# A planner's prices for VectorE and ScalarE, its page lines, and the order of a tail product

## The chip, the cores and the metric

The kernel runs on one core of one Trainium2 chip. The metric is the device time in microseconds of one execution; the median of several is given. The profile is taken by the hardware in one execution of its own.

## The reference

One decoder layer on a sequence of 512 tokens with 1024 features, all float32. What is computed, cut to its skeleton:

```python
h = rms_norm(x, mix_norm_g)
u, q, kv, nsa_g, merge_g = split(h @ w_in)
gate_pool, gate_nsa = split(sigmoid(merge_g))
y_pool = pooling_mixer(u) @ w_pool_out          # causal means over 2, 4, 8, 16 tokens
y_nsa = nsa_mixer(q, kv, sigmoid(nsa_g)) @ w_nsa_out   # compressed, selected and window attention
x = x + (gate_pool * y_pool + gate_nsa * y_nsa) @ w_out
h = rms_norm(x, ffn_norm_g)
gate_pre, val = split(h @ w_up)                 # 1024 -> 2 x 2816
x = x + (silu(causal_dwconv(gate_pre)) * val) @ w_down # 2816 -> 1024
```

## The kernel before

**Arithmetic.** Features lie on the 128 partitions, tokens along the free dimension. Every float32 operand of a large product is split in a high part (rounded, `hi`) and a rest (`lo`), and a product is three matmuls: hi x hi, hi x lo, lo x hi. `split` makes both by a ScalarE copy and a VectorE subtraction. `split_by_dma` makes the rest by a negated ScalarE copy and a DMA on POOL's queue that adds the original to it, and the high part by a second ScalarE copy.

**Stages.** Up to 38 us of the profile the q and k projections. From there to about 258 us attention runs in one stream of TensorE's program ("m") and the pooling, gates and their projections in another ("f"). Then, in one stream, the output projection of attention, `w_out`, and the feed-forward part, whose 22 feature tiles of 128 are called f: the first three plain, the others by `up_fast`, which replaces eight products of half size by seven (a Strassen-like scheme; `seven` prepares the seven weight operands by sums, `product` multiplies 256 token columns by four k tiles of 128). Parts of the down projection (`fill`) lie in between. The last eight down tiles are done two at a time by four calls of `seven_into`, p = 0 to 3, over the feature tiles 14 to 21: this is the tail. The moving operands of its products are `yq`, `yh` and `yl` of single tiles, or `zh` and `zl`, sums of pairs; k = 3 is the pair of the tiles 20 and 21, the last that `up_fast` makes. In `seven_into` the product with `h1` goes into a bank `bq`, the one with `h2` is added to a bank `by`. Each of them is then taken by VectorE into an output tile (`add`), and both banks are used again.

**Order.** Nothing is emitted as the program is written. `Plan` first records every operation (`note`), with a price (`price`: time on the engine `cost`, time after that until its result is there `tail`, bytes of a DMA `land`) and its dependences. `run` then simulates the engines with a list scheduler: for each engine, of the operations that could start within 0.12 us of the earliest, the one with the least key goes first. TensorE's operations stay in the order of their stream, and only the two streams are interleaved. DMAs share an assumed rate. Operations wait until the tiles that they open (`allocs`) have a buffer. Pages are 56 buffers of 128 x 512 float32, from which most tiles are taken; the staging tiles of `seven` (made by `soon`) are taken in a fixed order, a line, kept by `early`. `dues` then goes back over the plan and gives each operation the latest time at which it doesn't delay TensorE (`due`), which is the key of the next round. `search` does 12 rounds, and the plan with the least sum of four trial executions under other DMA assumptions is emitted; its order of instructions for each engine and its buffers are then fixed for the chip. All instructions are issued from one line of `emit`, so all carry the line L431 in the profile; tiles tell them apart.

Of the kernel before, what the change touches and what calls it, by code (L numbers as in the profile page):

```python
# [86 lines left out]
def _cols(x):  # L87
    n = 1
    for _, c in list(x.ap)[1:]:
        n *= c  # L90
    return n


class Op:
    __slots__ = ("i", "eng", "calls", "cost", "tail", "land", "deps", "succ", "allocs", "tiles", "stream", "left",
                 "ready", "start", "fin", "due", "hand", "port")

    def __init__(self, i, eng, stream):
        self.i, self.eng, self.stream = i, eng, stream
# [15 lines left out]
class Plan:  # L115
# [54 lines left out]
    def note(self, eng, method, a, kw):  # L170
        if self.open is None or self.open == "new":
            op = Op(len(self.ops), eng, self.stream)
            op.deps.update(o.i for o in self.after)
            self.ops.append(op)
            if self.open == "new":
                self.open = op
            if method == "transpose":
                op.cost += SWITCH
        else:
            op = self.open  # L180
            assert op.eng == eng
        outs = [a[0]] if a else []
        outs += [v for k, v in kw.items() if k in self.OUT and v is not None]
        ins = [v for v in a[1:] if hasattr(v, "tensor")]
        ins += [v for k, v in kw.items() if k not in self.OUT and hasattr(v, "tensor")]
        op.calls.append((method, a, kw))
        cost, tail, land = self.price(eng, method, outs, ins, a, kw)
        op.cost += cost
        op.port |= eng == "POOL" and method[:6] == "tensor" or eng == "DVE" and not any(
            x.tensor.name in self.psum for x in ins)  # L190
        op.tail = tail
        op.land = max(op.land, land)
        if kw.get("accum_op") is not None:
            ins.append(outs[0])
        for x, w in [(x, False) for x in ins] + [(x, True) for x in outs]:
            n = x.tensor.name
            if n not in self.tag:
                continue
            r = (0, 999, 0, 1 << 30) if n in self.psum and n not in self.fine else _span(x)
            past = list(self.writes.get(n, ()))  # L200
            if w:
                past += self.reads.get(n, ())
            for o, q in past:
                if o is not op and r[0] < q[1] and q[0] < r[1] and r[2] < q[3] and q[2] < r[3]:
                    op.deps.add(o.i)
            (self.writes if w else self.reads).setdefault(n, []).append((op, r))
            if not self.users[n]:
                op.allocs.append(n)
            if op not in self.users[n][-1:]:
                self.users[n].append(op)  # L210

    def price(self, eng, method, outs, ins, a, kw):
        n = max(_cols(x) for x in outs + ins)
        if method == "dma_start":
            x = outs[0]
            size = x.ap[0][1] * _cols(x) * 4 if hasattr(x, "ap") else 0
            return (0.87 if eng == "POOL" else 0.45), 0.0, size * (1.75 if kw.get("accum_op") is not None else 1.0)
        if eng == "PE":
            n = _cols(a[2])
            c = max(n / 2250.0 + (0.005 if n < 300 else 0.0), 0.109)  # L220
            return c * (2 if method == "matmul" and a[1].dtype == F32 else 1), 0.17, 0
        if eng == "ACT":
            c = 0.19 + n * 0.000835
            if any(_cols(x) == 1 for x in ins):
                c += 0.09
            if kw.get("accum_out") is not None:
                c += 0.19
            if a[2] in (AF.Sin,):
                c += 1.28
            return c, 0.0, 0  # L230
        if eng == "DVE":
            wide = [x for x in ins if _cols(x) > 1]
            if method == "tensor_tensor_reduce":
                return 0.24 + n * 0.00105, 0.0, 0
            if len(wide) > 1 or method == "tensor_reduce" or any(x.tensor.name in self.psum for x in wide):
                return 0.15 + n * (0.00105 if method != "scalar_tensor_tensor" else 0.00114), 0.0, 0
            return 0.2 + n * 0.00054, 0.0, 0
        if method == "memset":
            return 0.1 + n * 0.0008, 0.0, 0
        return 0.12 + n * 0.0023, 0.0, 0  # L240

    def run(self, key, reserve, land, rate=RATE, extra=EXTRA, fixed=None):
# [1 line left out]
        ahead = 0 if fixed else AHEAD  # L244
        engs = ("PE", "ACT", "DVE", "POOL", "SP")
        free = {t: [(0.0, "", i) for i in range(c)] for t, c in self.caps.items()}
        slot = self.slot if fixed else {}
        nxt = {t: 0 for t in self.FIFO}
        left = {n: len(u) for n, u in self.users.items()}
        clock = dict.fromkeys(engs, 0.0)  # L250
# [3 lines left out]
        pool = {e: [] for e in engs}  # L254
        heads = {}
        for o in ops:
            o.left, o.ready, o.start, o.hand = len(o.deps), 0.0, None, []
            if o.eng == "PE":
                heads.setdefault(o.stream, []).append(o)
            elif not o.left:  # L260
                pool[o.eng].append(o)
# [5 lines left out]
        def finish(o):  # L267
            for n in o.tiles:
                left[n] -= 1
                if not left[n]:  # L270
                    free[self.tag[n]].append((max(u.fin for u in self.users[n]) + 0.06, n, slot[n][1]))
            for s in o.succ:
                s.left -= 1
                s.ready = max(s.ready, o.start + o.cost if s.eng == o.eng and not o.land else o.fin + 0.06)
                if not s.left and s.eng != "PE":
                    pool[s.eng].append(s)

# [20 lines left out]
        def when(o):  # L298
            t, seen = o.ready, {}
            for n in o.allocs:  # L300
                g = self.tag[n]
                seen[g] = k = seen.get(g, 0) + 1
                f = free[g]
                if fixed:
                    past = [x[0] for x in f if x[1:] == slot[n]]
                    if not past:
                        return None
                    t = max(t, past[0])
                    continue
                if g in nxt and self.rank[n] != nxt[g] or n in self.early and self.early[n] != line[0]:  # L310
                    return None
                if len(f) < k + (0 if g != "pg" else ahead if n in self.early else reserve if o.stream == "f" else 0):
                    return None
                t = max(t, min(f)[0] if k == 1 else sorted(f)[k - 1][0])
            return max(t, clock[o.eng], port[0] if o.port and o.eng != port[1] else 0.0)
# [25 lines left out]
        while len(order) < len(ops):  # L341
# [9 lines left out]
            w, o = best  # L351
# [12 lines left out]
            else:  # L364
                pool[o.eng].remove(o)
            for n in o.allocs:
                g = self.tag[n]
                f = free[g]
                past = [x for x in f if x[1:] == slot[n]][0] if fixed else min(f)
                slot[n] = past[1:]  # L370
                f.remove(past)
                for u in self.users.get(past[1], ()):
                    u.hand.append(o)
                if g in nxt:
                    nxt[g] += 1
                if n in self.early:
                    line[0] += 1
            order.append(o)
            if not o.land:
                finish(o)  # L380
# [6 lines left out]
    def dues(self, order):  # L387
        lost, end, due = 0.0, 0.0, {}
        for o in order:
            if o.eng == "PE":  # L390
                lost += max(0.0, o.start - end)
                end = o.start + o.cost
                due[o.i] = o.start - lost + self.base
        for o in reversed(order):
            d = due.get(o.i, 1e9)
            for s in o.succ + o.hand:
                d = min(d, s.due - 0.06 - (o.fin - o.start))
            o.due = d

    def search(self, tries, reserve):  # L400
        for n, u in self.users.items():
# [33 lines left out]
def hybrid_layer(ctx: ExitStack, tc: tile.TileContext, found, first, xT, pos, par, cst, poolw, w1, wa, wb, wf,  # L435
# [695 lines left out]
        n = x.ap[1][1]  # L1131
        return bass.AP(tensor=x.tensor, offset=x.offset + n - 1, ap=[list(x.ap[0]), [-1, n]])

    def product(bank_, a, b, k0, nk=4):
        ah, al = a
        bh, bl = b
        for k in range(nk):
            c = slice(k * P, (k + 1) * P)
            with pl.unit():
                for j, (w, x) in enumerate(((ah, bh), (ah, bl), (al, bh))):  # L1140
                    PE.matmul(back(bank_[:, :H2]), w[:, c], back(x(k)), start=k0 and k == 0 and j == 0,
                              stop=k == nk - 1 and j == 2, skip_group_check=True)
# [61 lines left out]
    def seven_into(o0, o1, w, mv, nk, done, last):  # L1204
# [10 lines left out]

        def rest():
            bq = any_bank()
            product(bq, h1, mv(2, 0), True, nk)
            add(o1, HI, bq, -1)
            product(by, h2, mv(2, 1), False, nk)  # L1220
            add(o0, HI, by, 1)
            product(bx, a12, mv(1, 0), False, nk)
            add(o0, LO, bx, 1)
# [369 lines left out]
```

## Time and profile before

| what | value |
|---|---|
| median of 3 runs | 681.88 us (681.45 to 682.67) |
| the profiled execution | 682.61 us |
| its span | 680.7 us |
| TensorE busy | 675.9 us (99%), 4182 matmuls |
| VectorE, ScalarE busy | 515.4 us (1095), 451.8 us (848) |
| granted TensorE clock | 0.999 |

The span goes from the first to the last instruction of the program; the execution's time has 1.9 us more. PE is TensorE's matmul, PEld its weight load, DVE VectorE, ACT ScalarE, POOL GpSimd, SP SyncE, which issues most loads. Names such as `sl<-r` say output and input by the program's tiles. A matmul's duration overlaps the next one's, so whether TensorE waits is read from the distance between starts: 0.227 us for 512 columns and 0.118 us for 256 where nothing is waited for.

### The profile page before, as it was taken

The page shows a single profiled execution, that of the slowest core. Times are in us where ns is not written, and L with a number is a line of the kernel's source. Part 1 is how long each engine was busy: PE and PEld are TensorE (multiplying, and loading weights), DVE is VectorE, ACT ScalarE, POOL GpSimd, SP SyncE. Part 2 cuts the span into 40 slices and gives each one's busy share as a digit, 9 for nine tenths or more (in the row PEclk, how much of TensorE's full clock was granted, in tenths as well). Part 3 has the DMA queues.
Part 4 walks back from the last instruction along what each step waited for, and adds up shares of the span by engine and source line. Part 5 has one row for each costly group of instructions (what it writes and reads, how often), then busy time and mean ns, then how long its engine had stood idle before and what let it go on. Part 6 is the DMA issues. An engine that isn't in the chain of part 4 may idle for free.

```text
span 680.7 us, 11651 instructions
## 1 busy us (share of the span) xinstructions
PE 675.9 (99%) x4182; PEld 607.3 (89%) x4182; DVE 515.4 (76%) x1095; ACT 451.8 (66%) x848; POOL 117.4 (17%) x142
## 2 busy tenths in 40 slices
PE   9999999999999999999999999999999999999998
PEld 8898888888888888888888999999999999999997
DVE  6869878888888743876879977866677777888882
ACT  8565878777766653444758877866666667778770
POOL 0012211000111110000203432322222223222240
PEclk9999999999999999999999999999999999999999
DMA  8466995425556558736739798887677767878882
GB/s 304 145 167 166 268 250 141 109 63 155 125 125 155 143 120 274 281 126 231 186 87 234 139 224 214 176 215 168 155 164 188 185 163 167 187 165 193 185 175 92
DMA packets 50586, 119.28 MB, mean 175 GB/s; under 512 B 5856, under 2 KB 7904, under 8 KB 50528
## 3 DMA queue, kind: packets, MB, share of 16 engines
q0 software_dynamic: 18432, 40.90, 34.4%
q1 hardware_dynamic: 31808, 77.36, 34.0%
q8 instruction: 33, 0.54, 0.3%
q10 hardware_dynamic: 288, 0.27, 0.1%
q14 instruction: 25, 0.20, 0.1%
HBM read 70.27 MB, written 6.29 MB: 112 GB/s over the span
## 4 chain that ended last, share of the span: by engine, by line
PE 96%; DMA 2%; issue 1%; DVE 0%; POOL 0%; SPq 0%; POOLq 0%
PE mm L431 38%; PE tr L431 33%; PE sc L431 13%; PE av L431 13%; DMA sl<-r 1%; DMA wraw<-wa 0%; POOL sl L431 0%; DVE th L431 0%; DVE u L431 0%; DVE wraw L431 0%; DVE x L431 0%; SPq L431 0%; DVE whi L431 0%; POOLq L431 0%; DVE y L431 0%
## 5 line engine op out<-in xcount | busy, mean ns | idle before, releaser
L431 ACT ACTIVATE whi<-wraw 128x1024 fp32r<-128x1024 f32 (+1 forms) x89 | 90.4, 1019 | 66.9 <-issue 23.0
L431 DVE TENSOR_TENSOR wlo<-wraw,whi 128x1024 fp32r<-128x1024 f32 (+1 forms) x62 | 71.4, 1154 | 18.7 <-ACT whi L431 18.2
L431 POOL DMA_DIRECT2D sl<-r x46 | 40.0, 869 | 226.2 <-ACT sl L431 212.8
L431 PE MATMUL mm<-xh,whi 128*128 128x512 f32 x176 | 70.3, 400 | 0.1
L431 PE MATMUL mm<-xh,wlo 128*128 128x512 f32 x176 | 68.9, 391 | 0.0
L431 PE MATMUL mm<-xl,whi 128*128 128x512 f32 x176 | 68.8, 391 | 0.0
L431 POOL DMA_DIRECT2D wlo<-wraw x28 | 24.5, 876 | 246.9 <-ACT wlo L431 194.2
L431 PE MATMUL tr<-nh,whi 128*128 128x256 f32 x216 | 46.6, 282 | 0.0
L431 ACT ACTIVATE wlo<-wraw 128x1024 fp32r<-128x1024 f32 x28 | 29.5, 1059 | 24.2 <-PE mm L431 22.9
L431 ACT ACTIVATE pp<-pp,asm 128x128 f32<-128x128 f32 (+3 forms) x64 | 35.6, 558 | 13.9 <-DVE asm L431 13.3
L431 DVE SCALAR_TENSOR_TENSOR ft<-fg,pr,ft 128x511 f32<-128x511 f32 (+1 forms) x44 | 33.0, 750 | 12.7 <-ACT ft L431 11.8
L431 PE MATMUL tr<-nh,wlo 128*128 128x256 f32 x144 | 40.5, 282 | 0.0
L431 PEld LDWEIGHTS mm<-xh,wlo 128*128 128x128 f32 x176 | 33.0, 188 | 7.3
L431 PEld LDWEIGHTS mm<-xh,whi 128*128 128x128 f32 x176 | 33.1, 188 | 5.6 <-DVE u L431 0.5
L431 PEld LDWEIGHTS mm<-xl,whi 128*128 128x128 f32 x176 | 33.1, 188 | 5.0
L431 PEld LDWEIGHTS tr<-nh,whi 128*128 128x128 f32 x216 | 35.6, 188 | 0.0
L431 PE MATMUL sc<-yh,whi 128*128 128x512 f32 x91 | 35.5, 390 | 0.0
L431 PE MATMUL sc<-yl,whi 128*128 128x512 f32 x91 | 35.5, 390 | 0.0
L431 PE MATMUL sc<-yh,wlo 128*128 128x512 f32 x91 | 35.4, 389 | 0.0
L431 PE MATMUL tr<-tl,sh 128*128 128x256 f32 x113 | 31.8, 281 | 0.0
L431 ACT ACTIVATE sh<-wraw 128x512 fp32r<-128x512 f32 x44 | 27.4, 622 | 4.3 <-DVE wraw L431 4.1
L431 ACT ACTIVATE sl<-r 128x512 fp32r<-128x512 f32 x46 | 28.6, 622 | 2.0 <-DVE r L431 1.0
(451 smaller groups left out, 2261.5 us busy)
## 6 DMA issues: line engine op xcount, KB each, us to landing
wlo<-wraw POOLq DMA_DIRECT2D x28, 512.0 KB, 4.7
wraw<-wup SPq DMA_DIRECT2D x24, 512.0 KB, 4.0
sl<-r POOLq DMA_DIRECT2D x46, 256.0 KB, 4.5
wraw<-wf SPq DMA_DIRECT2D x22, 512.0 KB, 3.7
r<-wup SPq DMA_DIRECT2D x38, 256.0 KB, 5.2
sl<-s POOLq DMA_DIRECT2D x23, 256.0 KB, 4.6
sl<-wraw POOLq DMA_DIRECT2D x22, 256.0 KB, 4.5
wraw<-wout SPq DMA_DIRECT2D x8, 512.0 KB, 3.7
```

The source lines that it names most:

```text
L431: getattr(self.real[o.eng], method)(*a, **kw)
```

## The change

Three parts.

1. `price` for ScalarE and VectorE. Before, an operation held its engine for its whole duration and had no tail; a dependent one on the same engine could start when that cost was over. Now the cost is the step from one start to the next, about 0.1 (ScalarE) or 0.085 us (VectorE) shorter than the duration, and that rest is the tail. A dependent operation on the same engine starts 0.035 us after the end, TensorE's excepted. Operands of one column are priced each, and the custom reduction and the three-operand form are no longer priced apart.
2. Page lines. A tile is opened by any operation that meets no earlier access of it, not by the first recorded one alone, and once only (`got`). Operations that take a page of the line (`lined`) inherit in `dues` the earliest due time of later ones in the line.
3. `product` can be given its k tiles. In `seven_into`, where there is no earlier group's end to place (p = 0), the products with `h1` and `h2` do their first three k tiles each, then the fourth of each, and the subtraction from `o1` follows both.

The core of the diff:

```diff
-            if not self.users[n]:
+            if not met and n not in op.allocs:
                 op.allocs.append(n)
...
+        few = sum(_cols(x) == 1 for x in ins)
         if eng == "ACT":
-            c = 0.19 + n * 0.000835
-            if any(_cols(x) == 1 for x in ins):
-                c += 0.09
-            if kw.get("accum_out") is not None:
-                c += 0.19
+            c = 0.19 + n * 0.00085 + 0.095 * few
             if a[2] in (AF.Sin,):
                 c += 1.28
-            return c, 0.0, 0
+            if kw.get("accum_out") is not None:
+                return 0.30 + n * 0.0008, 0.2, 0
+            over = 0.115 if any(x.tensor.name in self.psum for x in ins) else 0.1
+            return c - over, over, 0
         if eng == "DVE":
             wide = [x for x in ins if _cols(x) > 1]
-            if method == "tensor_tensor_reduce":
-                return 0.24 + n * 0.00105, 0.0, 0
+            c = 0.155 + 0.06 * few
             if len(wide) > 1 or method == "tensor_reduce" or any(x.tensor.name in self.psum for x in wide):
-                return 0.15 + n * (0.00105 if method != "scalar_tensor_tensor" else 0.00114), 0.0, 0
-            return 0.2 + n * 0.00054, 0.0, 0
+                c += n * 0.00105
+            else:
+                c += n * 0.00054
+            return c - 0.085, 0.085, 0
...
-                s.ready = max(s.ready, o.start + o.cost if s.eng == o.eng and not o.land else o.fin + 0.06)
+                s.ready = max(s.ready, o.fin + 0.06 if s.eng != o.eng or o.land else o.start + o.cost if o.eng == "PE" else o.fin + 0.035)
...
+        line = 1e9
         for o in reversed(order):
             d = due.get(o.i, 1e9)
+            if o.lined:
+                d = min(d, line)
             for s in o.succ + o.hand:
                 d = min(d, s.due - 0.06 - (o.fin - o.start))
             o.due = d
+            if o.lined:
+                line = d
...
-            product(bq, h1, mv(2, 0), True, nk)
-            add(o1, HI, bq, -1)
-            product(by, h2, mv(2, 1), False, nk)
+            if last:
+                product(bq, h1, mv(2, 0), True, nk)
+                add(o1, HI, bq, -1)
+                product(by, h2, mv(2, 1), False, nk)
+            else:
+                for ks in (range(nk - 1), (nk - 1,)):
+                    product(bq, h1, mv(2, 0), True, nk, ks)
+                    product(by, h2, mv(2, 1), False, nk, ks)
+                add(o1, HI, bq, -1)
```

More of the change, by code (lines that the diff above doesn't have):

```diff
@@ L95 @@
     __slots__ = ("i", "eng", "calls", "cost", "tail", "land", "deps", "succ", "allocs", "tiles", "stream", "left",
-                 "ready", "start", "fin", "due", "hand", "port")
+                 "ready", "start", "fin", "due", "hand", "port", "lined")
     def __init__(self, i, eng, stream):
@@ L202, in note @@
                 past += self.reads.get(n, ())
-            for o, q in past:
-                if o is not op and r[0] < q[1] and q[0] < r[1] and r[2] < q[3] and q[2] < r[3]:
-                    op.deps.add(o.i)
+            met = [o for o, q in past if r[0] < q[1] and q[0] < r[1] and r[2] < q[3] and q[2] < r[3]]
+            op.deps.update(o.i for o in met if o is not op)
             (self.writes if w else self.reads).setdefault(n, []).append((op, r))
-            if not self.users[n]:
+            if not met and n not in op.allocs:
                 op.allocs.append(n)
@@ L246, in run @@
         free = {t: [(0.0, "", i) for i in range(c)] for t, c in self.caps.items()}
-        slot = self.slot if fixed else {}
+        slot, got = self.slot if fixed else {}, set()
         nxt = {t: 0 for t in self.FIFO}
@@ L256, in run @@
         for o in ops:
-            o.left, o.ready, o.start, o.hand = len(o.deps), 0.0, None, []
+            o.left, o.ready, o.start, o.hand, o.lined = len(o.deps), 0.0, None, [], False
             if o.eng == "PE":
@@ L300, in when @@
             for n in o.allocs:
+                if n in got:
+                    continue
                 g = self.tag[n]
@@ L366, in run @@
             for n in o.allocs:
+                if n in got:
+                    continue
+                got.add(n)
                 g = self.tag[n]
@@ L377, in run @@
                     line[0] += 1
+                    o.lined = True
             order.append(o)
@@ L1132, in back, with product @@
         return bass.AP(tensor=x.tensor, offset=x.offset + n - 1, ap=[list(x.ap[0]), [-1, n]])
-    def product(bank_, a, b, k0, nk=4):
+    def product(bank_, a, b, k0, nk=4, ks=None):
         ah, al = a
         bh, bl = b
-        for k in range(nk):
+        for k in ks or range(nk):
             c = slice(k * P, (k + 1) * P)
```

## The prediction

> **What bounds the kernel now.** I read the page first (shares, clock, chain of work that ended last), then the busy time by stretches, then the timeline at the few places where TensorE's busy time is shorter than the stretch.
>
> ```profile
> span 680.7 us, 11651 instructions
> PE 675.9 (99%) x4182; PEld 607.3 (89%) x4182; DVE 515.4 (76%) x1095; ACT 451.8 (66%) x848; POOL 117.4 (17%) x142
> PEclk9999999999999999999999999999999999999999
> PE 96%; DMA 2%; issue 1%; DVE 0%; POOL 0%; SPq 0%; POOLq 0%
> ```
>
> TensorE is busy 99% of the span at the full granted clock, and 96% of the last chain is its own. The change removes and adds no matmul, so only the time in which TensorE waits can be won. Where that is, the stretches say (columns: length, then busy time and count of PE, PEld, DVE, ACT, POOL, clock, DMA share, GB/s):
>
> ```profile
> 0.00:5.00 5.00, 3.75 (x17) 3.56 (x18) 1.18 (x5) 2.33 (x4) 0.41 (x5) 1.00 0.66 197
> 5.00:38.00 33.00, 33.00 (x191) 28.72 (x191) 26.23 (x70) 21.96 (x38) 1.00 (x1) 1.00 0.65 216
> 38.00:258.00 220.00, 219.81 (x1199) 188.70 (x1198) 174.23 (x518) 155.29 (x332) 28.19 (x34) 1.00 0.60 154
> 258.00:640.00 382.00, 382.00 (x2468) 349.38 (x2467) 289.48 (x458) 255.69 (x446) 79.18 (x92) 1.00 0.75 186
> 640.00:650.00 10.00, 9.85 (x83) 9.65 (x82) 9.31 (x16) 7.01 (x13) 2.44 (x3) 1.00 0.74 170
> 650.00:681.00 31.00, 27.53 (x233) 27.32 (x231) 14.94 (x31) 9.50 (x18) 6.19 (x8) 0.98 0.62 141
> ```
>
> In the 382 us from 258 to 640 TensorE is busy for 382.00. The stretch 38 to 258 misses 0.19, 640 to 650 misses 0.15. The first 5 us wait for the first loads (the first real matmul's, 0.45, quoted next), and the 3.47 missing from the last stretch are the last addition and the output's way out. Busy time hides part of a wait, because the 0.39 us of one matmul overlaps the next; so I go by distances between starts. In the timeline (start, duration, engine, what) these are the wait at the start and the three outside the two ends:
>
> ```profile
> 4.72 0.19 PEld L431 LDWEIGHTS tr<-whi,xh 128*128 128x128 f32 x1 [0.45 <-ACT xh L431]
> ...
> 177.73 0.69 DVE L431 TENSOR_TENSOR u<-mm,rb 128x512 f32<-128x512 f32 x1 [1.66 <-PE mm L431]
> 177.76 0.40 PE L431 MATMUL mm<-pml,pwh 128*128 128x512 f32 x1
> 177.99 0.40 PE L431 MATMUL mm<-pmh,pwl 128*128 128x512 f32 x1
> 178.47 0.51 PE L431 MATMUL mm<-xh,whi 128*128 128x512 f32 x1
> 178.82 0.40 PE L431 MATMUL mm<-xl,whi 128*128 128x512 f32 x1
> ...
> 203.49 0.39 PE L431 MATMUL mm<-pmh,pwl 128*128 128x512 f32 x1
> 203.99 0.50 PE L431 MATMUL mm<-yph,whi 128*128 128x512 f32 x1
> 204.33 0.40 PE L431 MATMUL mm<-ypl,whi 128*128 128x512 f32 x1
> ...
> 648.67 0.28 PE L431 MATMUL mm<-zl,sh 128*128 128x256 f32 x1
> 649.10 0.39 PE L431 MATMUL mm<-zh,sl 128*128 128x256 f32 x1
> 649.32 0.28 PE L431 MATMUL mm<-zh,sh 128*128 128x256 f32 x1
> ```
>
> A 512-column matmul normally starts 0.23 after the one before (177.76 to 177.99). Here 177.99 to 178.47 is 0.48 and the next step 0.35: 0.25 + 0.12 lost. At 203.49 it is 0.50 and 0.34: 0.27 + 0.11. Both times three matmuls of `mix` took one "mm" bank and the next user had to wait for VectorE to empty the other. A 256-column matmul takes 0.12; 648.67 to 649.10 is 0.43 and the next 0.22: 0.31 + 0.10 lost, waiting for a DMA. Together 0.37 + 0.38 + 0.41 = 1.16 us are to be won in the body.
>
> **The change, part by part.** (1) The prices. Rows that they stand against:
>
> ```profile
> 629.21 0.62 ACT L431 ACTIVATE sh<-s 128x512 fp32r<-128x512 f32 x1
> 629.73 0.62 ACT L431 ACTIVATE sl<-r 128x512 fp32r<-128x512 f32 x1
> 634.67 1.54 DVE L431 SCALAR_TENSOR_TENSOR ft<-fg,pr,ft 128x511 f32<-128x511 f32 x2
> 646.16 0.68 DVE L431 TENSOR_TENSOR x<-mm,x 128x512 f32<-128x512 f32 x1
> 646.76 0.68 DVE L431 TENSOR_TENSOR x<-tr,x 128x512 f32<-128x512 f32 x1
> ```
>
> ScalarE's 512-column copy lasts 0.62 but the next starts 0.52 later. The old price books 0.19 + 512 x 0.000835 = 0.62, the new one a step of 0.525 and an end of 0.625. VectorE's two-input operation lasts 0.68, the next starts 0.60 later: old 0.69, new 0.608 and 0.693. Where the second needs the first (the two `ft` operations, 1.54 together), the first's share is 1.54 - 0.75 = 0.79, if the second lasts the 0.75 that old (0.73) and new (0.75) come near to; old 0.73, new 0.753 + 0.035 = 0.79. So the new prices fit these rows better: the planner books 848 x 0.09 = 76 us less of ScalarE and 1095 x 0.085 = 93 us less of VectorE, counts from the page, sizes from the rows. No instruction becomes faster by that; only the order on the queues and the buffers taken change. TensorE's order after 258 us is one stream in program order and stays; between 38 and 258 two streams may interleave otherwise. Its own worth: gain at most the 0.75 of the two `mix` waits, loss bounded by new waits of the size just shown, about 0.4 each. I take 0: the wait behind `mix` was in the old plan too, since the end that VectorE gives back the bank (0.69) is the same in both prices.
>
> The Trainium skill, "VectorE: DVE Perf Modes", section "The DRAIN you can't avoid", says that the next operation does not start until the pipe is empty, and adds that one which is not held starts earlier. Read strictly, a step equals a duration, the old price is right and the new one books too little. The two independent additions at 646.16 and 646.76 say otherwise here: 0.60 apart, 0.68 long.
>
> (2) Page lines. Pages that must be handed out in a fixed order now inherit the due time of later ones, so a load of the next group's `r1`, `r2` that blocks the line goes ahead. On SP's queue it can pass a `wraw` load, whose users then get it later by one 0.4 us issue. Worth directly: 0, hidden by the landing-to-use distance of several us. If a load's cover is gone, the price is a wait like that at 649.10. On POOL's queue the DMAs are in order of their ScalarE copies and follow those. Taking a page by whichever part is written first (the new `met` test) moves no instruction by itself: 0, either side inside the same 0.4.
>
> (3) The tail. Rows around it:
>
> ```profile
> 638.61 0.28 PE L431 MATMUL mm<-zh,sh 128*128 128x256 f32 x1
> 639.68 0.28 PE L431 MATMUL mm<-zh,sh 128*128 128x256 f32 x1
> 640.03 0.28 PE L431 MATMUL av<-zh,sh 128*128 128x256 f32 x1
> 642.87 0.28 PE L431 MATMUL av<-zh,sh 128*128 128x256 f32 x1
> ...
> 638.82 0.69 DVE L431 TENSOR_TENSOR zl<-ta,zh 128x512 fp32r<-128x512 f32 x1
> 641.65 0.42 DVE L431 TENSOR_TENSOR x<-x,av 128x256 f32<-128x256 f32 x1 [0.54 <-PE av L431]
> 642.59 1.22 DVE L431 TENSOR_TENSOR wlo<-wraw,whi 128x1024 fp32r<-128x1024 f32 x1
> ...
> 638.04 0.68 DVE L431 TENSOR_TENSOR r<-r,r 128x512 f32<-128x512 f32 x1
> 640.13 0.62 ACT L431 ACTIVATE sl<-r 128x512 fp32r<-128x512 f32 x1
> 641.05 8.01 DMA sl<-r
> ```
>
> Before, the tenth matmul of the first z product (639.68) needs `zl` of the last pair, which ends at 638.82 + 0.69 = 639.51: 0.17 to spare, no wait. With nine matmuls of each product first, that k tile is needed at 638.61 + 18 x 0.118 = 640.73, with 1.2 to spare. By itself that wins 0. It gives ScalarE and VectorE 9 x 0.118 = 1.06 us in which the weights for the second tail product can go ahead: their `r` was ready at 638.72, but the copy started at 640.13, behind work for the last pair, and its accumulating DMA (issued 641.05, 8.01 us) is what TensorE awaited at 649.10. Started a microsecond earlier, that DMA lands before 648.67 and 0.41 goes; next late is nothing up to the end, since the stretch 650 onward has no body wait. This chain row is from the chain of work, the others from the timeline.
>
> What the part adds: the subtraction of `o1` now comes after both products, so VectorE has it and the addition of `o0` to do between about 641.3 and 642.87, where `by` is used again. 0.42 + 0.42 fit. Should the 1.22 of a weight's `wlo` go in between, the addition ends near 643.2 and TensorE waits 0.35, with the rest of its queue behind it. The six moved groups of three matmuls cost nothing: from 639.68 to 640.03, across the change of bank and product, is three steps of 0.12. I take -0.41 for this part, ends -0.41 and +0.35.
>
> Sum: 0 + 0 - 0.41. The profiled execution took 682.61 (span 680.7 and 1.9 around it), 0.73 over the median 681.88; it would become 682.2, and the median 681.5.
>
> **The rivals.** Change of under 0.2% (1.36 us) is about what a measurement of this kernel can't tell from none.
> - *All waits go.* Better fidelity also places a stream's work behind `mix`: 1.16 in the body and up to 0.45 before the first real matmul. That gives 680.3. Against: the first loads set the start, and nothing in the diff touches `mix`.
> - *The cushion goes.* The old plan booked ScalarE at 0.62 per copy where 0.52 were used, so every queue ran ahead of its plan. A group of the fast stage has, by its code, 17 ScalarE operations (10 for the weights, 4 copies of banks, 2 in `conv`, 1 for `y`): 17 x 0.095 = 1.6 us of cover for late landings. Landings of accumulating DMAs vary:
>
> ```profile
> DMA to landing us min/median/max: 3.2/4.5/8.7
> ```
>
>   With that cover gone a landing near 8 can stop TensorE for 0.41 as at 649.10. It decides when more than four do (4 x 0.41 = 1.64, less the 0.41 won, is 1.23); with six the time is 681.88 + 5 x 0.41 = 683.9. For it: one landing of 8.01 did so. Against: the landing of 8.7 did not, and 382 us ran without a wait.
> - *The tail was not binding, and the orders stay near enough the same:* 681.9.
> - *VectorE's steps do run to their ends when full.* In 640 to 650, where it is fullest, 16 operations would be 16 x 0.085 = 1.36 late: 683.2. The rows at 646 speak against it. This is the strict reading of the skill's page on VectorE above.
>
> **How the numbers follow.** Forecast 0.50 (681.5, own range 680.8 to 682.5), all waits go 0.18, cushion 0.20, tail not binding 0.10, steps to their ends 0.02. Faster by over 0.2%: 0.18; slower 0.22; within it 0.60. The range leaves out the far half of both outer cases: 680.3 to 683.9.
>
> **What would show it.** Right: no step over 0.2 between 256-column matmuls around 648; the first z product's starts in blocks of 9, 9, 3, 3; `sl<-r` of the second tail group issued before 640.5; 258 to 640 still full; the count of instructions unchanged. Wrong: TensorE waiting on `DMA sl` in the fast stage (cushion), on VectorE's `x` near 642.87 (tail), or a busy time in 38 to 258 short by over a microsecond (interleaving). A median outside 680.8 to 682.5 says that the re-pricing, taken as 0, decided.

## The result and the profile after

The changed kernel takes 685.96 us (median; 685.02 to 688.23), the kernel before, run beside it, 681.82 (680.89 to 683.0): a ratio of 1.0063, interval 1.0051 to 1.0075. It is slower by about 0.6%, where 681.5 was forecast. The profiled execution took 685.66, its span is 683.9, the granted clock 1.0. The two profiled executions are 3.05 apart and the medians 4.14, because that of before (682.61) was slower than its median; the stage readings below split the smaller difference.

The page of the changed kernel: span, busy times, and the chain that ended last by engine and by line.

```profile
span 683.9 us, 11665 instructions
PE 675.9 (99%) x4182; PEld 606.8 (89%) x4182; DVE 516.9 (76%) x1095; ACT 449.0 (66%) x848; POOL 117.3 (17%) x142
PE 95%; DVE 3%; issue 1%; ACT 0%; POOL 0%; DVEq 0%; POOLq 0%
PE mm L442 36%; PE tr L442 33%; PE av L442 13%; PE sc L442 13%; DVE qt L442 1%; DVE qp L442 1%; DVE kp L442 1%; DVE kc L442 0%; DVE w1s L442 0%; DVE kt L442 0%; DVE rt L442 0%; DVE vv L442 0%; ACT vv L442 0%; DVE four L442 0%; DVE x L442 0%
```

TensorE's work is the same 675.9 us; the span has grown by 3.2. The chain now runs through VectorE for 3% (0% before), and the tiles in it (`qt`, `qp`, `kp`, `kc`, `kt`) prepare q, k and the compressed keys (`kc`). The busy times by stretches say where (columns as before):

```profile
...
38.00:258.00 220.00, 216.23 (x1180) 184.89 (x1179) 176.54 (x517) 150.56 (x328) 26.32 (x32) 1.00 0.58 150
258.00:640.00 382.00, 382.00 (x2458) 348.88 (x2457) 285.32 (x452) 252.16 (x440) 78.38 (x91) 1.00 0.75 186
640.00:650.00 10.00, 10.00 (x84) 9.84 (x82) 9.96 (x20) 8.01 (x15) 2.58 (x3) 1.00 0.91 205
...
```

TensorE is short by 3.77 us in 38 to 258 (0.19 before), still full from 258 to 640, and full in 640 to 650. In finer stretches I add up, over every pair of successive matmuls, the distance between their starts less the median for that number of columns in the profile before. Loss after less loss before: 0 to 50 us -0.55; 50 to 90 us +4.97 (5.61 against 0.64); 90 to 260 us -0.92; 260 to 640 +0.07; from 640 on -0.41. Together 3.16, the delay of the last matmul. So the gains that the prediction looked for are there, and all of the loss lies in 40 us that it did not look at.

TensorE's waits there, in its timeline (start, duration, what, and in brackets the idle time and what ended it):

```profile
61.30 0.39 PE L442 MATMUL mm<-xh,wlo 128*128 128x512 f32 x1
62.40 0.63 PE L442 MATMUL tr<-cs,qp 128*128 128x128 f32 x4 [0.71 <-DVE kp L442]
68.31 0.39 PE L442 MATMUL mm<-xh,wlo 128*128 128x512 f32 x1
71.37 0.66 PE L442 MATMUL tr<-cs,qp 128*128 128x128 f32 x4 [2.67 <-DVE qp L442]
```

These are the third and fourth of the four transposes of q and k (`qk_transpose`), which need the `qp` and `kp` that VectorE has normalised and rotated. The step to the third is 1.10 instead of 0.23: 0.87 lost. To the fourth it is 3.06: 2.83 lost. Two smaller waits, 0.54 and 0.14 by starts, follow at 77 and 85 us. Why VectorE is late stands in its own timeline (xN is N instructions in a row, timed from the first start to the last end):

```profile
55.96 0.42 DVE L442 TENSOR_TENSOR kt<-tr,kt 64x256 fp32r<-64x256 f32 x1
56.41 0.42 DVE L442 TENSOR_TENSOR kp<-sc,small 128x256 f32<-128x256 f32 x1
56.87 0.42 DVE L442 TENSOR_TENSOR kt<-tr,kt 64x256 fp32r<-64x256 f32 x1
57.32 0.69 DVE L442 TENSOR_TENSOR qp<-av,small 128x512 f32<-128x512 f32 x1
57.93 0.41 DVE L442 TENSOR_TENSOR kp<-sc,small 128x256 f32<-128x256 f32 x1
58.37 1.39 DVE L442 TENSOR_TENSOR qt<-tr,qt 64x512 fp32r<-64x512 f32 x2
59.69 0.87 DVE L442 TENSOR_TENSOR kt<-tr,kt 64x256 fp32r<-64x256 f32 x2
60.59 0.29 DVE L442 TENSOR_TENSOR qp<-qp,gq 128x128 f32<-128x128 f32 x1
...
62.30 1.72 DVE L442 TENSOR_TENSOR kc<-mm,rb 64x256 f32<-64x256 f32 x4
64.06 0.29 DVE L442 TENSOR_TENSOR qp<-qp,gq 128x128 f32<-128x128 f32 x1
64.11 2.83 POOL L442 TENSOR_TENSOR kcb<-kc,pr 128x512 f32<-128x512 f32 x2 [2.21 <-DMA w<-w]
64.27 1.52 DVE L442 TENSOR_TENSOR kp<-kp,gkv 128x256 f32<-128x256 f32 x1
65.70 1.31 DVE L442 TENSOR_TENSOR rt<-qp,rope 128x64 f32<-128x64 f32 x1
```

Two things are seen. First, the steps. The new price books a step of 0.339 for a 256-column operation (0.155 + 256 x 0.00105 - 0.085) and 0.608 for 512. Where operations on 64 rows stand among the others, the steps are 55.96 to 56.41, 56.41 to 56.87, 56.87 to 57.32, 57.93 to 58.37, 59.69 to 60.14 (0.87 - 0.42 later) and 60.14 to 60.59: about 0.45 each, 0.11 over the booking. Inside each of two `qt` pairs (58.37, and one before these rows at 54.65) it is 0.70, 0.09 over. But 57.32 to 57.93 is 0.61, as booked. Six times 0.11 and twice 0.09 are 0.85 by 60.6, about the 0.87 that TensorE loses at 62.40. Second, at 64.27 and 65.70 two operations last 1.52 and 1.31; the same forms take 0.42 and 0.22 elsewhere. They read and write SBUF alone and meet the two `kcb` additions of GpSimd (64.11 to 66.94): 1.10 + 1.09 = 2.2 us late. The 0.85 had been paid at 62.40 already; what is left of the 2.83, some 0.6, is of the size of the long steps behind that wait: the four `kc` from 62.30 to 64.06 alone take 1.76 where four times 0.339 is 1.36. In the kernel before the same pair of additions fell on operations that read a PSUM bank:

```profile
61.69 2.88 POOL L431 TENSOR_TENSOR kcb<-kc,pr 128x512 f32<-128x512 f32 x2
61.92 1.39 DVE L431 TENSOR_TENSOR qt<-tr,qt 64x512 fp32r<-64x512 f32 x2
63.23 0.87 DVE L431 TENSOR_TENSOR kt<-tr,kt 64x256 fp32r<-64x256 f32 x2
64.13 0.69 DVE L431 TENSOR_TENSOR qp<-av,small 128x512 f32<-128x512 f32 x1
64.73 0.28 DVE L431 TENSOR_TENSOR qp<-qp,gq 128x128 f32<-128x128 f32 x1
```

The additions end at 64.57, the first operation in SBUF alone starts at 64.73, and none is held.

### The profile page after: what moved, and what is told of

It is laid out like the page before. It is cut to its first block, busy times and chain, and to the rows that moved or that the text cites. A ratio compares the mean times of both kernels' runs of the same rounds, so it can differ in the third digit from the quotient of the medians.

```text
span 683.9 us, 11665 instructions
## 1 busy us (share of the span) xinstructions
PE 675.9 (99%) x4182; PEld 606.8 (89%) x4182; DVE 516.9 (76%) x1095; ACT 449.0 (66%) x848; POOL 117.3 (17%) x142
## 4 chain that ended last, share of the span: by engine, by line
PE 95%; DVE 3%; issue 1%; ACT 0%; POOL 0%; DVEq 0%; POOLq 0%
PE mm L442 36%; PE tr L442 33%; PE av L442 13%; PE sc L442 13%; DVE qt L442 1%; DVE qp L442 1%; DVE kp L442 1%; DVE kc L442 0%; DVE w1s L442 0%; DVE kt L442 0%; DVE rt L442 0%; DVE vv L442 0%; ACT vv L442 0%; DVE four L442 0%; DVE x L442 0%
## 5 line engine op out<-in xcount | busy, mean ns | idle before, releaser
L442 ACT ACTIVATE pp<-pp,asm 128x384 f32<-128x384 f32 (+3 forms) x64 | 35.4, 555 | 17.8 <-DVE asm L442 17.6
```

Of the source, the lines that this page charges most:

```text
L442: getattr(self.real[o.eng], method)(*a, **kw)
```

## The experiments

The theory: the new prices book some VectorE steps too short, VectorE comes late, and its lateness moves SBUF work under GpSimd's additions. The rivals: the page lines; the tail; the collision alone; ScalarE's prices. Ratios are to the kernel before on the same chip.

### One part at a time

**e1, the prices alone.** Edit: the lines of the diff in `price` and the one line for `s.ready`; `allocs`, `lined` and `seven_into` as before.

> Only the prices are changed (with the 0.035 behind the end); page lines and tail order as before. Theory S (steps): VectorE operations on 64 partitions whose range changes from one to the next follow at their end (0.70 and 0.43 us in the traces), the new price books 0.61 and 0.34; VectorE is late from 55 us on, the four q and k transposes come too early in TensorE's order, and the delayed queue meets GpSimd's additions. Then this alone is as slow as the whole change: 685.5 to 686.5 us, with 4 us of waits before transposes between 60 and 78. Rival L (page lines cause it): 681.0 to 682.0, no such waits.

Measured 687.26, ratio 1.0076 (1.0063 to 1.0089), above the range that was expected. The whole loss is there with the first part alone. TensorE loses 0.87 and 2.81 before the third and fourth transposes. It also loses in the tail, where the order is the old one; TensorE's timeline:

```profile
643.48 0.28 PE L432 MATMUL mm<-zh,sh 128*128 128x256 f32 x1
644.42 0.39 PE L432 MATMUL mm<-zl,sh 128*128 128x256 f32 x1 [0.66 <-DVE zl L432]
```

The first matmul that needs `zl` starts 0.94 after the one before instead of 0.12.

**e2, the page lines alone.** Edit: `met`, `got`, `lined` and the inheritance in `dues`; prices and tail as before.

> Only the page lines and the opening of tiles are changed. Theory S: within 0.2% of before, 681 to 683, the stretch 52 to 78 as before. Rival L: 685 or more, with the waits of the changed kernel between 60 and 78.

Measured 682.88, ratio 1.0011 (1.0003 to 1.002). No wait between 52 and 78 us; the loss from 50 to 90 is 0.73. They are not the cause of the 0.6%, though the interval leaves them a loss of about 0.1%: in this plan's tail the wait at 648 is absent and another stands, 0.51 at 642.8 for `yl`.

**e3, the tail alone.** Edit: `ks` in `product` and the new branch of `seven_into`.

> Only the first tail product's order is changed. Both theories: within 0.2% of before. By the prediction's step -0.41: 681.4, no wait at 648; if the tail was not binding: the same as before and the wait still there.

Measured 682.22, ratio 0.9999 (0.999 to 1.0008). The wait at 648 is gone (TensorE's loss from 640 on is 0.11 instead of 0.52), but the time does not show the 0.4: it is smaller than the interval, 0.6 us each way.

**e6, prices and page lines.** Edit: only `product` and `seven_into` put back.

> Prices and page lines, but the first tail product in the old order. If the tail order was what kept the last pair's zl off the path under the new prices, a wait of 0.5 to 1 us for zl near the tenth matmul of the first z product comes and the time is 686.5 to 687.2; if it was the page lines, 685.5 to 686.2 and no such wait.

Measured 686.61, ratio 1.0063 (1.0049 to 1.0077): the time of the first case that was named, with the tail of the second. The waits in 55 to 90 are those of the whole change (0.83, 2.84, 0.54 by starts). In the tail the wait of e1 for `zl` is not there; what is left is 0.25 + 0.10 at 653.4 for the DMA into `sl`. So with the new prices the page lines, or the other plan that comes with them, take that wait away; the tail order on top of the prices alone was not run. In e14 below, which has both parts and ScalarE's old price, a wait for `zl` is there again (0.64 at 642.4). How much each part is worth on top of the other, times this close do not tell.

### The steps

**e4, 64-row operations booked to their end.** Edit, in the VectorE price of the whole change:

```diff
+            if any(x.ap[0][1] < P for x in outs + ins if hasattr(x, "ap")):
+                return c + 0.02, 0.0, 0
             return c - 0.085, 0.085, 0
```

> The whole change, but VectorE operations that touch fewer than 128 partitions are booked at their end plus 0.02 instead of a shorter step. Theory S: the transposes move later in TensorE's order and the 4.4 us of waits between 60 and 85 go, 1.16 us of before's waits stay away: 680.5 to 681.5. Theory P (GpSimd's additions alone hold VectorE, whatever the booking): two operations of over 1.2 us on VectorE remain and the time stays over 684.

Measured 682.77, ratio 1.001 (1.0002 to 1.0019): all but 0.1% of the loss is gone, but the time is over the 680.5 to 681.5 that was expected. The last two transposes in its timeline:

```profile
62.69 0.60 PE L444 MATMUL tr<-cs,qp 128*128 128x128 f32 x4
68.83 0.60 PE L444 MATMUL tr<-cs,qp 128*128 128x128 f32 x4
```

TensorE reaches them about as early as in the changed kernel (before, they start at 67.67 and 74.47), and neither waits. The earlier place is not the fault, then: with those steps booked at their length, the plan has VectorE's work ready for it, and no operation is held beside GpSimd. e4 cures the lateness and the collision at once; e9 below parts them.

**e12, the same edit again,** beside other kernels.

> The kernel with the 64-partition booking once more, for a second profile: its runs lay between 681.95 and 684.69, wider than those of before. If its order has lost cushion, this profile has another set of waits than the first one, in the stretch 258 to 650 and on DMAs; if only the clock at the start varies, the body has the 0.39 at 78 again and nothing else over 0.2.

Measured 683.0, ratio 1.0012 (1.0001 to 1.0023), so the 0.1% stays. The profile shows one more wait than e4's, 0.71 at 74.3 for `w1s`. In ScalarE's timeline two pairs of `w1s` copies (69.42 and 70.67) wait 0.45 and 0.53 for loads into `w`, which they don't in e4; the `qt` copies behind them start at 71.42 instead of 70.17, and VectorE's work follows those. So 70 to 80 us varies between executions with the landing of these loads; it is not shown that this makes the 0.1%.

**e8, steps by themselves.** A small kernel of independent VectorE additions in place of the layer; the first five rows below are each eight additions of 256 columns, by partitions from input to output: `full` all 128, `same` 0-63 to 0-63, `shift` 0-63 to 64-127, `swap` by turns 0-63 to 64-127 and back, `mixed` by turns 128 and 64 rows. `bankswap` is `swap` with one input in PSUM. `port` and `bankport` are twelve additions beside one GpSimd addition of 512 columns, with both inputs in SBUF and with one in PSUM.

> The layer is left out; VectorE alone does rows of equal additions of 256 columns: full (128 to 128 partitions), same (0-63 to 0-63), shift (0-63 to 64-127 always), swap (alternately 0-63 to 64-127 and back), mixed (128 and 64 in turn), bank and bankswap (one operand in a bank), then 12 beside a GpSimd addition of 512 columns, with operands in SBUF (port) and with one in a bank (bankport). Theory S: starts 0.33 to 0.34 apart in full, same, shift and bank; 0.42 to 0.45 in swap, mixed and bankswap. If few partitions were the reason: 0.43 in same and shift too. Collision: in port one or more additions last over 1 us, in bankport all 0.42.

VectorE's timeline, and GpSimd's two additions:

```profile
4.05 2.77 DVE L471 TENSOR_TENSOR full<-a,b 128x256 f32<-128x256 f32 x8 [3.05 <-DMA b<-xT]
6.74 2.76 DVE L471 TENSOR_TENSOR same<-a,b 64x256 f32<-64x256 f32 x8
9.51 2.77 DVE L471 TENSOR_TENSOR shift<-a,b 64x256 f32<-64x256 f32 x8
12.20 3.45 DVE L471 TENSOR_TENSOR swap<-a,b 64x256 f32<-64x256 f32 x8
15.66 2.77 DVE L471 TENSOR_TENSOR mixed<-a,b 128x256 f32<-128x256 f32 x8
...
21.09 3.47 DVE L471 TENSOR_TENSOR bankswap<-pt,b 64x256 f32<-64x256 f32 x8
25.19 5.17 DVE L471 TENSOR_TENSOR port<-a,b 128x256 f32<-128x256 f32 x12
...
30.88 0.68 DVE L482 TENSOR_TENSOR go<-a,b 128x512 f32<-128x512 f32 x1
31.59 4.06 DVE L471 TENSOR_TENSOR bankport<-pt,b 128x256 f32<-128x256 f32 x12
25.35 1.37 POOL L484 TENSOR_TENSOR kport<-go,b 128x512 f32<-128x512 f32 x1 [24.91 <-DVE go L482]
31.64 1.26 POOL L484 TENSOR_TENSOR kbankport<-go,b 128x512 f32<-128x512 f32 x1 [4.92 <-DVE go L482]
```

With 0.42 for the last one, eight in 2.77 are seven steps of 0.336; eight in 3.45, seven of 0.433. `mixed` at 0.336 was expected long: a change of row count costs nothing. What costs is a change of where input and output lie: in `swap` every time, in `shift` and `same` never after the first. Whether it is the starts themselves or the distance between them, `swap` changes both and can't tell. One step speaks for the starts: `go` and the first `bankport` both go from all 128 partitions to all 128, and yet `bankport` begins only after the end of `go` (31.59 against 30.88 + 0.68 = 31.56); what had moved is the start in PSUM, which `bankswap` had last read from partition 64 on. `port` takes 1.11 more than `bankport`: one addition in SBUF alone is held until GpSimd's ends.

The Trainium skill, "VectorE: DVE Perf Modes", section "Two Vector instructions with no wait between them", has this condition: an instruction is held until the earlier ones have finished when an input or the output starts in another group of 32 partitions than the last one in the same memory. All of e8's rows agree with it. The Trainium skill's "SBUF — State Buffer", section "SBUF: two separate sides", calls the ports that VectorE and GpSimd share an exclusive lock for the whole instruction, which binds VectorE where it has two SBUF inputs; `port` and `bankport` agree.

**e7 and e10, a planner that knows of held steps.** Both add 0.1 to a VectorE start in `run`, e7 where the partition ranges of output and first input differ from those of the operation before, e10 where the distance from output to input does:

```diff
+            op.rows = tuple(_span(x)[:2] for x in outs[:1] + ins if _cols(x) > 1)[:2]       # e7
+            op.rows = tuple(_span(x)[0] - _span(outs[0])[0] for x in ins[:1])               # e10
...
-            return max(t, clock[o.eng], ...)
+            return max(t, clock[o.eng] + (0.1 if o.eng == "DVE" and o.rows != rows[0] else 0.0), ...)
```

> The whole change, and the planner adds 0.1 us on VectorE wherever an operation's partition ranges differ from those of the operation before. Theory S: as with the 64-partition booking, no wait before the transposes, GpSimd's additions beside bank reads or alone: 680.5 to 682.8. Rival: something else made VectorE late, the waits between 60 and 78 stay over 2 us in sum and the time over 684.

> The whole change, and the planner adds 0.1 us on VectorE where the distance from input to output partitions differs from that of the operation before, which is what the additions alone showed. If steps booked right are enough: waits before the q and k transposes under 0.3 in sum, 681.0 to 682.5. If the collision comes whenever VectorE is a little late against GpSimd: one or more operations over 1.2 us and over 683.5.

Measured e7 684.62, 1.004 (1.0027 to 1.0052); e10 684.39, 1.0029 (1.0018 to 1.004). Less than the whole loss, more than e4. In e10 the waits before the transposes of q and k are gone, but other operations meet GpSimd's additions, and TensorE loses 0.58 and 1.00 before the products with `w1s` at 73.6 and 75.7; VectorE's and GpSimd's timelines:

```profile
71.72 1.87 DVE L446 TENSOR_TENSOR w1s<-w,w1s 128x256 fp32r<-128x256 f32 x2
73.50 1.78 DVE L446 TENSOR_TENSOR kcs<-kcb,kcs 128x512 fp32r<-128x512 f32 x1
71.84 2.90 POOL L446 TENSOR_TENSOR kcb<-kc,pr 128x512 f32<-128x512 f32 x2 [3.09 <-DVE kc L446]
```

In e7 one `kp` lasts 3.00 at 62.82, beside two additions in a row. Neither rule is the one that fits e8 (e7's books `mixed` too long; e10's, if it is the starts that count, misses steps that keep the distance and move both), and a planner with better steps still lets the collision happen by chance. e4's rule isn't e8's either (`same` has 64 rows and short steps); it fits here where the operations on 64 rows move from one half of the partitions to the other.

### The collision

**e5, the `kcb` additions taken from GpSimd,** in the changed kernel's own order of instructions; the added constant is left out:

```diff
-                POOL.tensor_add(b..., kc..., pe[...])
+                ACT.activation(b..., kc..., AF.Copy)
```

> The changed kernel's order and buffers are kept instruction for instruction; only the four additions on GpSimd (kcb) are ScalarE copies at the same places, which leaves out the addition of the block embedding. Theory S with collision: the two VectorE operations that last 1.52 and 1.31 us become 0.42 and 0.22, the 2.84 us wait at 68 shrinks by about 2.2, the 0.88 wait at 61 stays: 683.3 to 684.3 us. If the wrong steps alone make the waits: 685.5 or more. If the collision alone does: 681.5 or less and the wait at 61 gone too.

Measured 685.39, ratio 1.0055 (1.0043 to 1.0068): the time misses what was expected, the mechanism does not. TensorE's waits from the timeline:

```profile
63.14 0.63 PE L442 MATMUL tr<-cs,qp 128*128 128x128 f32 x4 [0.65 <-DVE kp L442]
69.91 0.66 PE L442 MATMUL tr<-cs,qp 128*128 128x128 f32 x4 [0.47 <-DVE qp L442]
81.94 0.75 PE L442 MATMUL tr<-w1s,kcs 128*128 128x256 f32 x4 [1.41 <-DVE w1s L442]
```

The fourth transpose loses 0.63 instead of 2.83. But ScalarE takes 1.10 for each such copy, and the work behind it waits: 0.73 at 71.7 and 1.58 at 80.1 are new. The substitute was not free.

**e9, the same additions cut to two columns,** on GpSimd and in the same order, so that nothing is added to another engine; what follows reads `kc` itself:

```diff
+                POOL.tensor_add(kc[:, 0, 2*a:2*a+2], kc[:, 0, 2*a:2*a+2], pe[:, i, 8*a:8*a+2])
```

> The changed kernel's order and buffers again, instruction for instruction, but each of the four GpSimd additions touches two columns of kc instead of making a 512-column tile (the rest of the block embedding's addition is left out), and what follows reads kc. GpSimd is as good as gone, and no other engine gets more work. Theory S with collision: no VectorE operation over 1.2 us, the wait at 68 shrinks from 2.84 to 0.5 to 0.7, the one at 61 stays at 0.8 to 0.9, and nothing takes its place: 683.2 to 684.2 us. If the wrong steps alone make the waits: 685.5 or more.

Measured 684.22, ratio 1.0028 (1.0018 to 1.0038). The timeline:

```profile
62.76 0.63 PE L442 MATMUL tr<-cs,qp 128*128 128x128 f32 x4 [0.66 <-DVE kp L442]
69.57 0.66 PE L442 MATMUL tr<-cs,qp 128*128 128x128 f32 x4 [0.47 <-DVE qp L442]
```

By starts 0.82 and 0.64 are lost instead of 0.87 and 2.83: the collision is 2.2 us of the second wait. In time it is 1.0063 - 1.0028 = 0.35%, 2.4 us; the other 0.28%, 1.9 us, stays without any collision (in e9 no VectorE operation is held). So neither the late steps nor the collision alone is the loss.

**e11, e10 with the `kcb` additions on VectorE** (`DVE.tensor_add` in place of `POOL.tensor_add`).

> As the one before, and the four additions of the block embedding are VectorE's instead of GpSimd's (2.8 us more on VectorE, nothing left to collide). If the collision is what makes the re-priced plan fragile: no operation over 1.2 us and 680.8 to 682.3, below the version with GpSimd. If VectorE's load is the limit here: waits before the transposes of over 1 us and 683 or more.

Measured 683.07, ratio 1.0013 (1.0004 to 1.0021), no operation held, no wait over 0.31 us by starts in 55 to 90, but 0.49 at 377 for `yl`. Without an engine to collide with, the same planner is 1.3 us faster than e10, though VectorE has four additions more.

### Which price

**e13, VectorE's old price in the whole change,** ScalarE's new one; **e14, the other way round.**

> The whole change, but VectorE's prices are the old ones (whole duration on the engine, no tail); ScalarE's are the new ones. If VectorE's price alone put the transposes too early: they come at 54, 59, 67 and 74 as before, no operation over 1.2 us, 681.0 to 682.5. If ScalarE's price does it too: 684 or more.

> The whole change, but ScalarE's prices are the old ones; VectorE's are the new ones. If VectorE's price alone does it: waits of over 2 us in sum between 55 and 85, 684 to 687. If it needs both: under 683.

Measured e13 683.14, 1.0016 (1.0007 to 1.0025); e14 683.58, 1.0025 (1.0016 to 1.0034). Both lie between the cases that were named; I had expected e14 to keep more. The last two transposes stand at 68.24 and 75.75 in e13, at 63.38 and 73.91 in e14, at 62.40 and 71.37 in the changed kernel. Each price alone costs 1.2 to 1.7 us, the two together 4.1; a chance collision is in both (`qp` lasts 1.45 in e13, `kp` 1.52 in e14). In 50 to 90 us TensorE loses 1.05 in e13 and 2.59 in e14 (0.64 before, 5.61 after), so in that stretch VectorE's price counts for more, but it isn't alone; e13's loss is in 90 to 260 (3.20 against 2.59 before), where three waits behind `mix` are back. The intervals of the two times overlap. A rival that these runs don't exclude: every change of a price makes `search` find another plan, and plans may differ by a few tenths of a per cent for no reason that the edit names; only e5 and e9 keep the order.

No version ran faster than the kernel before; of those with new prices e4, e11 and e12 come nearest, at 0.1% over it. Why they are not below it, with the waits at `mix` and 648 gone, is open. Their profiles lose between 70 and 85 us, where the waits vary, and e11's also at 377. In e4's profiled execution TensorE's last matmul even starts 0.48 earlier than in that of before, although its first 10 us lose 0.87 more; the median of its 12 runs doesn't show that, and no run settles it.

## Why the prediction was wrong

**The tail, -0.41: right in the mechanism, too small to be measured.** The starts come in blocks of 9, 9, 3 and 3, as TensorE's timeline shows at the first matmul of each:

```profile
642.19 0.28 PE L442 MATMUL mm<-zh,sh 128*128 128x256 f32 x1
643.25 0.28 PE L442 MATMUL av<-zh,sh 128*128 128x256 f32 x1
644.32 0.28 PE L442 MATMUL mm<-zh,sh 128*128 128x256 f32 x1
644.67 0.28 PE L442 MATMUL av<-zh,sh 128*128 128x256 f32 x1
```

The wait at 648 went, and the wait for `by` that was put at +0.35 did not come. The sign "`sl<-r` issued before 640.5" was badly chosen, an absolute time in a kernel whose middle had moved. "By itself that wins 0" of the later need of `zl` was right for the old plan, which had 0.17 to spare; under the new prices e1, with the old order, loses 0.82 + 0.11 there, and e14, with the new order, 0.64.

**The `mix` waits, 0.75, as the upper rival had it:** TensorE's loss from 90 to 260 fell from 2.59 to 1.67.

**Page lines, 0:** held to 0.1% (e2).

**The prices, "I take 0": the step that failed.** Its bounds were a gain of 0.75 and a loss of new waits of about 0.4 each; the waits that came are 0.87 and 2.83. Three things were wrong in it.
- "So the new prices fit these rows better" was read from rows at 629 to 647, where operations on all 128 partitions follow each other and steps are indeed 0.60 for 0.68. The operations on 64 rows that stand in the stretch where the streams interleave, 0.45 against 0.339 booked, were not looked at. The fence shows the fit, not where it ends. The rule of the Trainium skill's "VectorE: DVE Perf Modes", section "The DRAIN you can't avoid", was set aside rightly for independent additions that lie alike (`full` in e8: 0.336 apart, 0.42 long); the held case stands in the next section of the same page and was not drawn on.
- The rival "steps do run to their ends when full" got 0.02 and was placed in 640 to 650, all 16 operations or none. The truth is in between: some steps do, and where they are frequent they add up to 0.85 in six microseconds.
- A loss was bounded by the size of waits seen before. But GpSimd's `kcb` additions last 1.4 each, beside VectorE work whose order the planner was about to change, and the bound for that had to come from these rows: two held operations, 2.2.

**The rival "the cushion goes"** had the right idea and the wrong place. The old price booked 0.085 too much for most VectorE steps and about the right length for the held ones (0.69 against 0.70, 0.42 against 0.45), so VectorE could run ahead of its plan, and a plan that was wrong about some steps did little harm. That is argued from the prices; e13's 1.05 in 50 to 90 fits it, though one `qp` is held there too. I looked for that cushion's loss in ScalarE and late DMAs from 258 to 640; it went in VectorE from 50 to 75, and from 258 to 640 not one wait came. The sign named for being wrong by interleaving, a busy time in 38 to 258 short by over a microsecond, came at 3.77, and the median outside 680.8 to 682.5 said, as written, that the re-pricing decided; e1 confirms it. One sign of being right failed without any meaning for the time: the instructions are 11665 instead of 11651, while those of each compute engine are as many as before.

## What to carry to other kernels

When a scheduler's prices are made tighter, check them on the rows of the stretch where its order can change, one row for each shape and partition pattern; a fit on regular rows says nothing of the others, and an even overestimate can be what hides them. In an order fixed ahead, a small lateness has a fixed cost only until it moves an instruction beside another user of an exclusive resource: look up what each neighbour engine runs there, and take that instruction's length, or the sum of those in a row, as the bound.

## What the runs showed of the hardware

- VectorE's next addition of 256 columns starts 0.336 us after one of 0.42 when input and output start at the partitions where those of the one before did, and 0.433 after it when that changes; the number of rows, 64 or 128, doesn't matter (e8).
- A VectorE operation with both inputs in SBUF is held for about 1.1 us beside a GpSimd addition of 512 columns (1.37 us), and one lasts 3.00 instead of 0.42 beside two such additions in a row (e7); with one input in PSUM it is not held at all (e8, and the rows at 64 us before and after).
- TensorE's start differs between executions. In e3's profile the first large matmuls run at little more than half the rate, in that of the kernel before they do not, and the granted clock reads 1.00 in both; first e3's timeline, then the other's:

```profile
5.22 0.63 PE L431 MATMUL tr<-whi,xh 128*128 128x512 f32 x1
5.64 0.41 PE L431 MATMUL sc<-whi,xh 128*128 128x256 f32 x1
```

```profile
5.17 0.40 PE L431 MATMUL tr<-whi,xh 128*128 128x512 f32 x1
5.41 0.28 PE L431 MATMUL sc<-whi,xh 128*128 128x256 f32 x1
```

  A 512-column step is 0.42 in e3 and 0.24 in the other, up to 7 us into the span. TensorE's loss in the first 10 us is 2.0 to 3.1 over the profiles here, so differences under 1 us between two single profiles say little until that part is taken off.
